# Batched x·yᵀ on one core: PSUM copies of 4 banks and a last load in one piece

## The chip, the core and the metric

The kernel runs on one core of a Trainium2 chip. The metric is the device time of one execution in microseconds (us). The kernel before took 305.55 us, the median of three runs (304.52 to 305.66). The execution that the profiler recorded has a span of 303.9 us from its first to its last event.

## The reference

```python
def setup_inputs():
    batch, n_heads, seq_t, seq_s, channels = 8, 12, 512, 512, 64
    # x: [8, 12, 512, 64] fp32, y: [8, 12, 512, 64] fp32

def reference(x, y):
    return np.einsum('bhtc,bhsc->bhts', x, y).astype(np.float32)
```

For each of the 96 heads the product of a 512x64 matrix with the transpose of another is formed. The inputs are 25 MB, the output is 101 MB.

## The kernel before

The heads are taken in 12 load groups of 8. In a group x and y are each a block of 128 rows of 8 KB. A loaded group is turned into bf16 (`compress`), x is spread into buffers that are zero elsewhere (`mix`), both are transposed on VectorE (`transposes`), and `result` multiplies, copies the product out of PSUM and returns its store. There are 48 output tiles of 2 MB (128 partitions x 4096 fp32).

All large buffers, the loaded groups and the output tiles alike, come from one pool of five slots, taken in turn: whoever takes a slot waits until the one that had it five turns earlier is done with it.

```python
    slots = ctx.enter_context(tc.tile_pool(name="slots", bufs=SLOTS))          # SLOTS = 5
    pm3pool = ctx.enter_context(tc.tile_pool(name="pm3psum", bufs=2, space=bass.MemoryType.PSUM))
    pm2pool = ctx.enter_context(tc.tile_pool(name="pm2psum", bufs=1, space=bass.MemoryType.PSUM))

    def load(g):
        both = slot()
        for src, dst in ((xv[g], both[:, :R * C]), (yv[g], both[:, R * C:])):
            cuts = (0, P) if g < NG - 1 else (0, P - 16, P - 12, P - 8, P - 4, P)
            for lo, hi in zip(cuts[:-1], cuts[1:]):
                nc.sync.dma_start(dst[lo:hi], src[lo:hi])
        loaded[g] = both
```

Eleven groups are loaded with one DMA for x and one for y. The last is loaded with five DMAs each: rows 0 to 111, and four times 4 rows.

```python
    def result(o):
        i, h = divmod(o, 2)
        xT, yT = made[i]
        otf = slot()
        ot = otf.rearrange("p (r s) -> p r s", s=S)
        for k, n in ((0, 3), (3, 3), (6, 2)):
            pm = (pm3pool if n == 3 else pm2pool).tile([P, n, S], fp32, name=f"pm{n}")
            for j in range(n):
                nc.tensor.matmul(
                    pm[:, j, :], xT[:, k + j, h, :], yT[:, h * S:(h + 1) * S], start=True, stop=True
                )
            copy(nc.vector if o % 4 == 3 else nc.scalar, ot[:, k:k + n, :], pm)
        # ... transposes or mix for a later tile
        return lambda: nc.sync.dma_start(ov[i, h], otf)
```

[...] a tile fills eight banks[...]. Of four tiles ScalarE copies three and VectorE one.

```python
        for g in range(SLOTS):
            load(g)
        for k in range(0, K * E * D, 64):                       # K * E * D = 1024
            nc.vector.memset(zeroed[0][:, k:k + 64], 0.0)
            nc.gpsimd.memset(zeroed[1][:, k:k + 64], 0.0)
        stores = []
        for g in range(NG):                                     # NG = 12
            compress(g)
            mix(g // 2, [nc.gpsimd] * 4, (g % 2,))
            if g in (2, 4):
                transposes(g // 2 - 1)
            if g < 5:
                load(g + SLOTS)
            elif g in (5, 7, 9):
                stores.append(result(len(stores)))
            elif g in (6, 8):
                load(g // 2 + 7)
        for store in stores:
            store()
        for o in range(len(stores), 4 * NG):
            result(o)()
```

Three output tiles are thus made while the loads still run. Their stores are issued after the last load, all from SyncE's queue, and from then on each tile is stored when it is made.

Of the kernel before, what the change touches and what calls it, by code (L numbers as in the profile page):

```python
# [1 line left out]

# [4 lines left out]


@with_exitstack
def kernel(  # L10
    ctx: ExitStack,
    tc: tile.TileContext,
    x: bass.AP,
    y: bass.AP,
    out: bass.AP,
):

    nc = tc.nc
    B, H, T, C = x.shape  # L30
    _, _, S, _ = y.shape
    P = 128
    G = 8
    Q = P // G
    R = T // Q
    NG = B * H // G
    K = 8
    E = R // K
    D = 32
    SLOTS = 5  # L40
    fp32 = mybir.dt.float32
    bf16 = mybir.dt.bfloat16
    u32 = mybir.dt.uint32
    COPY = mybir.ActivationFunctionType.Copy
    assert C == 2 * D and S == T and R == D and Q * 2 == D

    xv = x.rearrange("b h t c -> (b h t c)").rearrange("(g p n) -> g p n", p=P, n=R * C)
    yv = y.rearrange("b h t c -> (b h t c)").rearrange("(g p n) -> g p n", p=P, n=R * C)
    ov = out.rearrange("b h t s -> (b h t s)").rearrange(
        "(o u h q n) -> o h q u n", u=2, h=2, q=Q * E, n=K * S  # L50
    )

    const = ctx.enter_context(tc.tile_pool(name="const", bufs=1))
    kept = ctx.enter_context(tc.tile_pool(name="kept", bufs=NG))
    slots = ctx.enter_context(tc.tile_pool(name="slots", bufs=SLOTS))
    tpool = ctx.enter_context(tc.tile_pool(name="tpool", bufs=3))
    pm3pool = ctx.enter_context(tc.tile_pool(name="pm3psum", bufs=2, space=bass.MemoryType.PSUM))
    pm2pool = ctx.enter_context(tc.tile_pool(name="pm2psum", bufs=1, space=bass.MemoryType.PSUM))

    loaded, inputs, mixed, made = {}, {}, {}, {}  # L60
    zeroed = [const.tile([P, K * E * D], u32, name=f"xb{half}") for half in range(2)]
    in_front = [nc.vector, nc.gpsimd, nc.vector, nc.scalar]
    FIRST = NG // 2

    def copy(engine, dst, src):
        if engine is nc.scalar:
            nc.scalar.activation(dst, src, COPY)  # L67
        else:
            engine.tensor_copy(dst, src)  # L69

    def slot():
        return slots.tile([P, K * S], fp32, name="slot")

    def load(g):
        both = slot()
        for src, dst in ((xv[g], both[:, :R * C]), (yv[g], both[:, R * C:])):
            cuts = (0, P) if g < NG - 1 else (0, P - 16, P - 12, P - 8, P - 4, P)
            for lo, hi in zip(cuts[:-1], cuts[1:]):
                nc.sync.dma_start(dst[lo:hi], src[lo:hi])  # L79
        loaded[g] = both  # L80

    def compress(g):

        both = loaded.pop(g)
        xk = kept.tile([P, R, C], bf16)
        nc.scalar.activation(xk.rearrange("p r c -> p (r c)"), both[:, :R * C], COPY)  # L86
        inputs[g] = xk
        ys = both[:, R * C:].rearrange("p (r c) -> p r c", c=C)
        for half in range(2):
            yb = kept.tile([P, R // 2 * D], u32, name=f"yb{half}")  # L90
            yv2 = yb.bitcast(bf16).rearrange("p (j c w) -> p j w c", j=R // 2, w=2)
            for ch in range(2):
                copy(
                    in_front[2 * half + ch],
                    yv2[ch * 64:(ch + 1) * 64],
                    ys[half * 64:(half + 1) * 64, :, ch * D:(ch + 1) * D].rearrange(
                        "p (j w) c -> p j w c", w=2
                    ),
                )
            mixed[2 * g + half] = yb  # L100

    def mix(i, engines, halves=(0, 1)):

        g, half = divmod(i, 2)
        xk = inputs[g]
        xv2 = zeroed[half].bitcast(bf16).rearrange("p (k e c u) -> p k e c u", k=K, e=E, u=2)
        for ch in halves:
            for u in range(2):
                lo = half * 64 + u * D
                copy(  # L110
                    engines[2 * ch + u],
                    xv2[(2 * ch + u) * D:(2 * ch + u + 1) * D, :, :, :, u],
                    xk[lo:lo + D, :, ch * D:(ch + 1) * D].rearrange("p (e k) c -> p k e c", k=K),
                )

    def transposes(i):
        xb, yb = zeroed[i % 2], mixed.pop(i)
        xT = tpool.tile([P, K * D * E], u32)
        nc.vector.transpose(  # L119
            xT.rearrange("p (k r e) -> p k e r", k=K, e=E),  # L120
            xb.rearrange("p (k e c) -> p k e c", k=K, e=E),
        )
        yT = tpool.tile([P, D * R // 2], u32)
        nc.vector.transpose(  # L124
            yT.rearrange("p (r j) -> p j r", r=D), yb.rearrange("p (j c) -> p j c", c=D)
        )
        made[i] = (xT.bitcast(bf16).rearrange("p (k h m) -> p k h m", k=K, h=2), yT.bitcast(bf16))

    def result(o):

        i, h = divmod(o, 2)
        xT, yT = made[i]
        otf = slot()
        ot = otf.rearrange("p (r s) -> p r s", s=S)
        for k, n in ((0, 3), (3, 3), (6, 2)):
            pm = (pm3pool if n == 3 else pm2pool).tile([P, n, S], fp32, name=f"pm{n}")
            for j in range(n):
                nc.tensor.matmul(  # L138
                    pm[:, j, :], xT[:, k + j, h, :], yT[:, h * S:(h + 1) * S], start=True, stop=True
                )  # L140
            copy(nc.vector if o % 4 == 3 else nc.scalar, ot[:, k:k + n, :], pm)
        if h == 0 and i + 2 < 2 * NG:
            transposes(i + 2)
        elif h == 1 and FIRST <= i + 4 < 2 * NG:
            mix(i + 4, [nc.scalar if o % 4 == 3 else nc.vector] * 4)
        return lambda: nc.sync.dma_start(ov[i, h], otf)

    with tc.manual_schedule():
        for g in range(SLOTS):
            load(g)  # L150
        for k in range(0, K * E * D, 64):
            nc.vector.memset(zeroed[0][:, k:k + 64], 0.0)  # L152
            nc.gpsimd.memset(zeroed[1][:, k:k + 64], 0.0)  # L153
        stores = []
        for g in range(NG):
            compress(g)
# [15 lines that stand above are left out]
# [1 line left out]
_INS = ['x', 'y']  # L173
_OUTS = [((8, 12, 512, 512), 'float32')]


# [23 lines left out]
```

## Time and profile before

| what | value |
|---|---|
| time, median of 3 | 305.55 us |
| span of the profiled execution | 303.9 us |
| granted TensorE clock, mean | 0.71 |
| ScalarE busy | 221.5 us |
| VectorE busy | 181.3 us |
| TensorE busy | 146.2 us |
| GpSimd busy | 59.1 us |
| moved by DMA | 125.93 MB, 414 GB/s over the span |
| time from issue to landing, stores (median) | 19.6 us |

In the profile a group of instructions is named by its line, engine and operation, then output<-input with shapes, the count, the busy time and the mean of one, and after the second bar the idle time of that engine just before these instructions with what ended it. The helper `copy` is one line for several uses (L67 on ScalarE, L69 on the other engines), so its groups are told apart by tile names and shapes: `slot<-pm` is a copy out of PSUM, `yb<-slot` and `xb<-xk` belong to the preparation. SPq is SyncE's queue of DMA issues: L79 issues loads and L146 stores. In rows by stage the columns are the stretch, its length, the busy time of PE, PEld, DVE, ACT and POOL with the number of instructions, then the granted clock, the mean busy share of the 16 DMA engines and the GB/s that they moved. A DMA engine counts as busy as long as it has a packet under way, however long that takes.

### The profile page before, as it was taken

To read this page: it belongs to the slowest core of one execution; us is meant where nothing else is said; L and a number is where in the kernel's file an instruction comes from. 1 tells how busy PE (TensorE), PEld (TensorE's weight loads), DVE (VectorE), ACT (ScalarE), POOL (GpSimd) and SP (SyncE) were. 2 spreads that over 40 slices of the span, in tenths; PEclk is the share of its full clock that TensorE was granted. 3 is DMA by queue.
4 is the path that set the end of the run, shared out by engine and by line. 5 is a ranking of instruction groups with operands and counts; after the bars stand their busy time and mean duration, and the time that the engine had idled before them with its cause. 6 is when DMAs were issued, how large, how long until landed. Compare 5 with 4: busy or idle time off the path is not lost.

```text
span 303.9 us, 1432 instructions
## 1 busy us (share of the span) xinstructions
PE 146.2 (48%) x384; PEld 46.5 (15%) x384; DVE 181.3 (60%) x160; ACT 221.5 (73%) x169; POOL 59.1 (19%) x56
## 2 busy tenths in 40 slices
PE   0004044225648457574757467565575477475000
PEld 0001011001212112121212112121121122121000
DVE  1568895909997493883947919569196461502300
ACT  4566599975998978979789888798896977184000
POOL 2899999945000000000000000000000000000000
PEclk9999555555995985776675965778857965776655
DMA  7999999999999999999999999999999999999995
GB/s 289 426 424 422 424 421 423 360 294 437 426 427 429 418 436 423 429 430 425 434 427 421 438 418 427 434 423 434 429 423 434 426 425 429 424 429 431 421 440 250
DMA packets 10409, 125.93 MB, mean 414 GB/s; under 512 B 1184, under 2 KB 1184, under 8 KB 1184
## 3 DMA queue, kind: packets, MB, share of 16 engines
q1 hardware_dynamic: 10400, 125.83, 99.0%
q8 instruction: 3, 0.05, 0.1%
q14 instruction: 6, 0.05, 0.0%
HBM read 25.17 MB, written 100.66 MB: 414 GB/s over the span
## 4 chain that ended last, share of the span: by engine, by line
DMA 62%; ACT 17%; DVE 8%; issue 4%; PE 1%; DVEq 1%; SPq 0%; ACTq 0%
DMA out_dram<-slot 49%; ACT slot L67 12%; DMA slot<-in_y_dram 11%; DVE slot L69 5%; DMA slot<-in_x_dram 3%; ACT xk L86 2%; ACT xb L67 2%; DVE yb L69 2%; ACT yb L67 1%; PE pm L138 1%; DVE xT L119 1%; DVE yT L124 1%; DVEq L195 1%; SPq L79 0%; DVEq L69 0%
## 5 line engine op out<-in xcount | busy, mean ns | idle before, releaser
L138 PE MATMUL pm<-yT,xT 128*128 128x512 bf16 x384 | 146.2, 521 | 133.0 <-ACT slot L67 74.5
L67 ACT ACTIVATE slot<-pm 128x1536 f32<-128x1536 f32 (+1 forms) x108 | 133.4, 1311 | 39.3 <-DMA out_dram<-slot 27.9
L69 DVE COPY slot<-pm 128x1536 f32<-128x1536 f32 (+1 forms) x36 | 54.6, 1572 | 73.0 <-DMA out_dram<-slot 40.6
L138 PEld LDWEIGHTS <-xT 128*128 128x128 bf16 x384 | 46.5, 121 | 231.8 <-issue 197.5
L119 DVE STREAM_TRANSPOSE xT<-xb 128x1024 uint32<-128x1024 uint32 x24 | 49.4, 2056 | 4.7 <-PE pm L138 3.1
L67 ACT ACTIVATE xb<-xk 32x1024 bf16<-32x1024 bf16 x36 | 48.1, 1337 | 0.8
L69 DVE CAST yb<-slot 64x1024 bf16<-64x1024 f32 x24 | 31.9, 1328 | 23.5 <-DMA slot<-in_y_dram 23.3
L69 POOL COPY xb<-xk 32x1024 bf16<-32x1024 bf16 x24 | 38.1, 1586 | 1.2
L86 ACT ACTIVATE xk<-slot 128x2048 bf16<-128x2048 f32 x12 | 22.9, 1910 | 9.9 <-DMA slot<-in_x_dram 9.4
L69 DVE COPY xb<-xk 32x1024 bf16<-32x1024 bf16 x36 | 26.1, 725 | 0.4
L124 DVE STREAM_TRANSPOSE yT<-yb 128x512 uint32<-128x512 uint32 x24 | 25.5, 1062 | 0.0
L69 POOL CAST yb<-slot 64x1024 bf16<-64x1024 f32 x12 | 19.7, 1643 | 11.5 <-DMA slot<-in_y_dram 10.9
L67 ACT ACTIVATE yb<-slot 64x1024 bf16<-64x1024 f32 x12 | 16.0, 1329 | 5.6 <-DMA slot<-in_y_dram 5.4
L86 ACT ACT_TABLE_LOAD x1 | 1.3, 1283 | 0.7 <-PEq L184 0.7
L152 DVE MEMSET xb<- 128x64 uint32 x16 | 1.2, 112 | 0.8 <-PEq L184 0.8
L153 POOL MEMSET xb<- 128x64 uint32 x16 | 1.4, 151 | 0.3 <-POOLq L184 0.3
L184 POOL MEMSET const-float32-0.0<- 128x1 f32 x1 | 0.1, 98 | 0.2 <-issue 0.2
L184 POOL MEMSET const-float32-1.0<- 128x1 f32 x1 | 0.1, 98 | 0.0
L184 POOL MEMSET const-bfloat16-1.0<- 128x1 bf16 x1 | 0.1, 98 | 0.0
L184 POOL MEMSET const-uint8-127<- 128x1 uint8 x1 | 0.1, 98 | 0.0
## 6 DMA issues: line engine op xcount, KB each, us to landing
out_dram<-slot SPq DMA_DIRECT2D x48, 2048.0 KB, 19.6
slot<-in_x_dram SPq DMA_DIRECT2D x11, 1024.0 KB
slot<-in_y_dram SPq DMA_DIRECT2D x11, 1024.0 KB, 19.9
slot<-in_x_dram SPq DMA_DIRECT2D x1, 896.0 KB
slot<-in_y_dram SPq DMA_DIRECT2D x1, 896.0 KB, 11.2
slot<-in_x_dram SPq DMA_DIRECT2D x4, 32.0 KB
slot<-in_y_dram SPq DMA_DIRECT2D x4, 32.0 KB
```

The source lines that it names most:

```text
L67: nc.scalar.activation(dst, src, COPY)
L69: engine.tensor_copy(dst, src)
L86: nc.scalar.activation(xk.rearrange("p r c -> p (r c)"), both[:, :R * C], COPY)
L119: nc.vector.transpose(xT.rearrange("p (k r e) -> p k e r", k=K, e=E), xb.rearrange("p (k e c) -> p k e c", k=K, e=E),)
L124: nc.vector.transpose(yT.rearrange("p (r j) -> p j r", r=D), yb.rearrange("p (j c) -> p j c", c=D))
L138: nc.tensor.matmul(pm[:, j, :], xT[:, k + j, h, :], yT[:, h * S:(h + 1) * S], start=True, stop=True)
L152: nc.vector.memset(zeroed[0][:, k:k + 64], 0.0)
L153: nc.gpsimd.memset(zeroed[1][:, k:k + 64], 0.0)
L184: nc = _bacc.Bacc("TRN2", target_bir_lowering=False, num_devices=1)
L195: with _tile.TileContext(nc) as tc:
```

## The change

It has three parts. The output tile leaves PSUM in two copies of four banks instead of three copies of 3, 3 and 2 banks, with one PSUM pool of two buffers in place of two pools with three buffers, so that there are fewer and larger copies. VectorE sets its buffer to zero in 4 fills of 256 columns instead of 16 of 64 (GpSimd keeps its 16), which makes 20 in all. And the last load group is loaded like the others, with one DMA of 128 rows for x and one for y, in place of the ten pieces.

```diff
-    pm3pool = ctx.enter_context(tc.tile_pool(name="pm3psum", bufs=2, space=bass.MemoryType.PSUM))
-    pm2pool = ctx.enter_context(tc.tile_pool(name="pm2psum", bufs=1, space=bass.MemoryType.PSUM))
+    pmpool = ctx.enter_context(tc.tile_pool(name="pmpsum", bufs=2, space=bass.MemoryType.PSUM))
 ...
     def load(g):
         both = slot()
-        for src, dst in ((xv[g], both[:, :R * C]), (yv[g], both[:, R * C:])):
-            cuts = (0, P) if g < NG - 1 else (0, P - 16, P - 12, P - 8, P - 4, P)
-            for lo, hi in zip(cuts[:-1], cuts[1:]):
-                nc.sync.dma_start(dst[lo:hi], src[lo:hi])
+        nc.sync.dma_start(both[:, :R * C], xv[g])
+        nc.sync.dma_start(both[:, R * C:], yv[g])
         loaded[g] = both
 ...
-        for k, n in ((0, 3), (3, 3), (6, 2)):
-            pm = (pm3pool if n == 3 else pm2pool).tile([P, n, S], fp32, name=f"pm{n}")
-            for j in range(n):
+        for k in range(0, K, 4):
+            pm = pmpool.tile([P, 4, S], fp32)
+            for j in range(4):
                 nc.tensor.matmul(
                     pm[:, j, :], xT[:, k + j, h, :], yT[:, h * S:(h + 1) * S], start=True, stop=True
                 )
-            copy(nc.vector if o % 4 == 3 else nc.scalar, ot[:, k:k + n, :], pm)
+            copy(nc.vector if o % 4 == 3 else nc.scalar, ot[:, k:k + 4, :], pm)
 ...
-        for k in range(0, K * E * D, 64):
-            nc.vector.memset(zeroed[0][:, k:k + 64], 0.0)
-            nc.gpsimd.memset(zeroed[1][:, k:k + 64], 0.0)
+        for half, engine, part in ((0, nc.vector, 256), (1, nc.gpsimd, 64)):
+            for k in range(0, K * E * D, part):
+                engine.memset(zeroed[half][:, k:k + part], 0.0)
```

## The prediction

> **What bounds the kernel now.** I first read the busy shares on the page, then the 40 slices with the DMA and GB/s rows.
>
> ```profile
> PE 146.2 (48%) x384; PEld 46.5 (15%) x384; DVE 181.3 (60%) x160; ACT 221.5 (73%) x169; POOL 59.1 (19%) x56
> ...
> DMA  7999999999999999999999999999999999999995
> GB/s 289 426 424 422 424 421 423 360 294 437 426 427 429 418 436 423 429 430 425 434 427 421 438 418 427 434 423 434 429 423 434 426 425 429 424 429 431 421 440 250
> DMA packets 10409, 125.93 MB, mean 414 GB/s; under 512 B 1184, under 2 KB 1184, under 8 KB 1184
> ...
> HBM read 25.17 MB, written 100.66 MB: 414 GB/s over the span
> ```
>
> No compute engine is above 73%, while the DMA row is 9 in 38 of 40 slices. The span is set by moving 125.83 MB at some 425 GB/s: 125.83 MB / 0.425 = 296 us of the 303.9. What can be won at all lies in the four slices that fall short: the first and the last, and the two in the middle with 360 and 294 GB/s. In those two the DMA row still says 9: the DMA engines are occupied but move less. That is the line that decides this case.
>
> Next, the table by stage around that dip (columns: busy time of PE, PEld, DVE, ACT, POOL, then granted clock, DMA share, GB/s):
>
> ```profile
> 54.00:58.00 4.00, 0.00 (x0) 0.00 (x0) 3.97 (x3) 3.87 (x4) 3.84 (x3) 0.50 1.02 393
> 58.00:60.00 2.00, 0.90 (x3) 0.34 (x3) 1.99 (x3) 2.00 (x2) 1.73 (x1) 0.50 1.04 299
> 60.00:62.00 2.00, 2.00 (x6) 0.61 (x5) 0.68 (x1) 1.98 (x3) 1.90 (x3) 0.50 1.15 229
> 62.00:64.00 2.00, 0.74 (x2) 0.15 (x1) 0.00 (x0) 1.98 (x2) 1.22 (x1) 0.50 0.92 184
> 64.00:66.00 2.00, 0.00 (x0) 0.00 (x0) 0.00 (x0) 1.69 (x2) 0.00 (x0) 0.50 0.99 365
> 66.00:68.00 2.00, 0.00 (x0) 0.00 (x0) 0.68 (x1) 0.81 (x1) 0.65 (x1) 0.50 0.99 406
> ...
> 76.00:300.00 224.00, 127.90 (x341) 40.63 (x340) 130.96 (x109) 167.40 (x134) 0.00 (x0) 0.72 1.01 428
> 300.00:303.90 3.90, 0.00 (x0) 0.00 (x0) 0.00 (x0) 0.00 (x0) 0.00 (x0) 0.50 0.19 80
> ```
>
> From 54 to 68 us the rate falls to 184 GB/s and comes back. Against 425 GB/s each row loses (1 - rate/425) x its length: 0.30 + 0.59 + 0.92 + 1.13 + 0.28 + 0.09 = 3.3 us of full transfer. What runs then is shown by SyncE's own timeline, which issues every transfer:
>
> ```profile
> 54.27 1.74 SPq L79 DMA_DIRECT2D slot<-in_x_dram  x5
> 56.06 6.65 SPq L79 DMA_DIRECT2D slot<-in_y_dram  x5
> 63.31 2.64 SPq L146 DMA_DIRECT2D out_dram<-slot  x3
> ```
>
> This is the last load group, the one in ten pieces. SyncE needs until 62.7 us to issue the pieces, and the first store, whose data has been in SBUF since 40.6 us, is only issued at 63.31. The trace's DMA packet records add the cause of the low rate. A row of 8 KB takes 0.31 us (median) in all loads before; of the 224 packets of the two 112-row transfers, nearly all take 0.42 to 1.03 us, mean 0.55, from 57.4 until 65 us. Then four engines still have 8 KB rows of the small pieces until 68.4 us, while the other twelve start the first store at 64.9.
>
> [...] 72 transfers x 16 + 8 pieces x 4 = 1184, which is the count of packets under 512 B above. [...]
>
> **The change part by part.** *1. The copies out of PSUM.* From the groups with shapes kept apart (the number after "busy us" is the mean ns of one):
>
> ```profile
> L67 ACT ACTIVATE slot<-pm 128x1536 f32<-128x1536 f32 x72 | 100.7, 1450 | 39.3 <-DMA out_dram<-slot 27.9 <-PE pm L138 4.0 <-DVE slot L69 2.9
> L67 ACT ACTIVATE slot<-pm 128x1024 f32<-128x1024 f32 x36 | 37.2, 1034 | 0.0
> L69 DVE COPY slot<-pm 128x1536 f32<-128x1536 f32 x24 | 41.0, 1751 | 73.0 <-DMA out_dram<-slot 40.6 <-PE pm L138 32.4
> L69 DVE COPY slot<-pm 128x1024 f32<-128x1024 f32 x12 | 14.6, 1214 | 0.0
> ...
> L152 DVE MEMSET xb<- 128x64 uint32 x16 | 1.2, 112 | 0.8 <-PEq L184 0.8
> ```
>
> A bank costs 1450 - 1034 = 416 ns on ScalarE and 537 ns on VectorE. A copy of 4 banks should take 1450 + 416 = 1.87 us on ScalarE and 2.29 us on VectorE. A tile goes from 3.93 to 3.73 us on ScalarE (36 tiles: 7 us less busy) and from 4.72 to 4.58 us on VectorE (12 tiles: 1.7 us less). Against it, there are two PSUM buffers instead of three, so TensorE fills 4 banks while the other 4 are emptied: 4 matmuls at the slower spacing seen, 0.43 us, are 1.7 us, still under the copy's 1.87. A store lasts 100.66 MB / 48 / 0.428 = 4.9 us per tile, longer than any copy of a tile. The waits above show that the copies already wait for stores (40.6 us on VectorE, 27.9 on ScalarE). All of part 1 therefore lies beside the transfers: 0 us.
>
> *2. The zeros.* VectorE's 16 small fills (1.2 us) become 4, and GpSimd keeps 16. VectorE then waits for the first y until 8.1 us. 0 us.
>
> *3. The last load group whole.* It removes eight transfers and puts 128 rows on 16 engines again. At 0.31 us a row, 8 rows of x and 8 of y take 4.95 us per engine: from 57.4 to 62.4 us instead of 64.9 on twelve engines and 68.2 on four. SyncE issues x and y by 55 us and can issue two stores right after, so each engine goes from the last load row to the first store row without a gap. Twelve engines gain 2.5 us, four gain 5.8 us; weighted, (12 x 2.5 + 4 x 5.8) / 16 = 3.3 us, the same as the table's loss.
>
> Does it stay won? The third store's tile leaves ScalarE at about 61.3 us, the fourth can be copied when the first store has landed (62.4 + 4.9 + 1, about 68.3) and takes 4.6 us: ready at 73 us. The three stores before it keep the engines busy until 62.4 + 3 x 4.9 = 77 us. The margin is 4 us, then it grows. At the end the last store is issued at 283.7 us, long before its turn, so the tail is a pure drain, and the gain comes out there. What the whole program gains depends on which engines end last: the twelve give 2.5, the four up to 5.8. The packet records show the engines' last completions between 300.6 and 302.95 us, and my attempt to follow engines through the records suggests that the four late ones are among the last. I take 3.5 us, a little above the mean.
>
> Sum: 0 + 0 + 3.5. 305.55 - 3.5 = 302.0 us.
>
> **The rivals.** *A: the dip is only shifted.* If the first stores after the load find no finished tile, the engines run dry at 73 us instead. For it: only three tiles are made ahead, and the fourth has 4 us of margin. Against it: slots and copies have that margin and VectorE, which copies it, idles before. If true, 0 to 2 us gain, 304 us. *B: two PSUM buffers of 4 banks make compute the bound.* For it: TensorE waits for PSUM already (74.5 us on ScalarE's copies). Against it: 4.2 us per tile even with a handoff of 0.2 per copy is below 4.9, and the order of ScalarE's work in four tiles (3 x 3.73 + 4 x 1.34 = 16.5 us) is below 4 x 4.9. If true, the DMA row would fall below 9 in the middle: 306 to 312 us. *C: the pieces were good for the tail.* They give twelve engines 14 rows instead of 16, 0.62 us less each; if those are the slow engines, the whole load gives that back. This is inside my sum for the twelve already and leaves at least 2.5 us.
>
> **Range and chances.** The low end takes 5 us of gain (four late engines set the end): 300.6. The high end takes 1.7 (some of A, plus the spread of the runs before, 304.52 to 305.66): 303.8. Faster by 2% needs under 299.4, a gain of 6.1 us, more than the whole dip; chance 0.05. Slower by 2% needs B; 0.01. Within 2%: 0.94.
>
> **What would show it.** Right: slices 8 and 9 of the GB/s row at about 425 and no ten-piece load; stores issued from 55 us; 72 transfers x 16 = 1152 packets under 512 B; ScalarE copies of 2048 elements near 1.87 us; a first store landing near 68 us. Wrong: a low GB/s slice somewhere between 73 and 90 us (A), DMA digits of 8 or less in the middle (B), or a last slice much emptier than 250 GB/s (C).

## The result, and the profile after

The changed kernel takes 302.0 us (median of 6 runs, 301.59 to 302.08) against 305.32 us; the ratio is 0.9893, with a 95% interval of 0.9879 to 0.9906. By the 2% mark that is the same time, and yet a clear gain of 3.3 us. The span of the profiled execution went from 303.9 to 300.3 us.

The same rows of the page, after (DMA busy tenths, GB/s in 40 slices, packets, totals):

```profile
DMA  7999999999999999999999999999999999999994
GB/s 282 430 422 421 420 423 422 421 432 443 420 432 438 417 434 437 421 437 434 420 437 434 423 432 432 423 443 426 421 450 419 426 439 423 419 437 428 426 434 194
DMA packets 10375, 125.92 MB, mean 419 GB/s; under 512 B 1152, under 2 KB 1152, under 8 KB 1152
...
HBM read 25.17 MB, written 100.66 MB: 419 GB/s over the span
```

The two slices of 360 and 294 GB/s are now 421 and 432, and nothing has dipped in their place. The DMA digits have hardly changed: they were 9 in the dip and are 9 now. Only the GB/s row shows the difference. The small packets are 32 fewer, four for each of the eight pieces.

By stage, over the same stretches (columns as before: PE, PEld, DVE, ACT, POOL, clock, DMA share, GB/s):

```profile
54.00:58.00 4.00, 0.00 (x0) 0.00 (x0) 3.97 (x3) 3.87 (x4) 3.88 (x3) 0.68 1.02 426
58.00:60.00 2.00, 0.56 (x2) 0.25 (x2) 1.99 (x3) 2.00 (x2) 1.96 (x1) 0.50 1.01 418
60.00:62.00 2.00, 2.00 (x6) 0.55 (x4) 0.56 (x1) 1.98 (x2) 1.93 (x2) 0.50 1.05 434
62.00:64.00 2.00, 0.76 (x3) 0.24 (x2) 0.63 (x1) 1.98 (x2) 1.70 (x2) 0.92 1.05 446
...
76.00:296.00 220.00, 123.70 (x336) 39.92 (x334) 126.09 (x92) 162.39 (x99) 0.00 (x0) 0.71 1.01 430
```

And SyncE's timeline around the last load, then the groups of the copies and of VectorE's zeros:

```profile
54.19 0.33 SPq L74 DMA_DIRECT2D slot<-in_x_dram  x1
54.57 0.42 SPq L75 DMA_DIRECT2D slot<-in_y_dram  x1
55.04 23.12 SPq L142 DMA_DIRECT2D out_dram<-slot  x6
```

```profile
L65 ACT ACTIVATE slot<-pm 128x2048 f32<-128x2048 f32 x72 | 131.1, 1876 | 40.0 <-DMA out_dram<-slot 31.6 <-PE pm L134 3.5 <-DVE yb L67 2.6
L67 DVE COPY slot<-pm 128x2048 f32<-128x2048 f32 x24 | 53.8, 2285 | 70.3 <-DMA out_dram<-slot 49.0 <-issue 19.8 <-PE pm L134 1.5
...
L149 DVE MEMSET xb<- 128x256 uint32 x4 | 1.1, 272 | 0.9 <-PEq L180 0.9
```

The last load is issued at the same time as before, 54.2 us, but it takes 0.8 us to issue instead of 8.4, and the first store follows at 55.04 instead of 63.31. In the DMA packet records the first rows of the first store start between 62.0 and 62.9 us on all 16 engines; before it was 64.6 to 65.0 us on twelve and 67.4 to 68.2 us on four. (These times are in the clock of the lines above; the packet times in the prediction lie about 0.24 us higher, which cancels in its differences.)

### The profile page after: what moved, and what is told of

It reads as the page before. It is cut to its first block, busy times and chain, and to the rows that moved or that the text cites. A ratio compares the mean times of both kernels' runs of the same rounds, so it can differ in the third digit from the quotient of the medians.

```text
span 300.3 us, 1359 instructions
## 1 busy us (share of the span) xinstructions
PE 143.4 (48%) x384; PEld 46.3 (15%) x384; DVE 180.8 (60%) x136; ACT 219.2 (73%) x133; POOL 59.3 (20%) x56
## 4 chain that ended last, share of the span: by engine, by line
DMA 49%; ACT 13%; DVE 5%; issue 4%; PE 1%; DVEq 1%; ACTq 0%
DMA out_dram<-slot 49%; ACT slot L65 10%; DVE slot L67 4%; ACT xb L65 2%; PE pm L134 1%; DVEq L191 1%; ACT xk L82 1%; DVE yb L67 0%; ACT yb L65 0%; DVE yT L120 0%; DVEq L67 0%; ACTq L65 0%
## 5 line engine op out<-in xcount | busy, mean ns | idle before, releaser
L134 PE MATMUL pm<-yT,xT 128*128 128x512 bf16 x384 | 143.4, 519 | 132.5 <-ACT slot L65 78.1
L65 ACT ACTIVATE slot<-pm 128x2048 f32<-128x2048 f32 x72 | 131.1, 1876 | 40.0 <-DMA out_dram<-slot 31.6
L67 DVE COPY slot<-pm 128x2048 f32<-128x2048 f32 x24 | 53.8, 2285 | 70.3 <-DMA out_dram<-slot 49.0
L67 DVE CAST yb<-slot 64x1024 bf16<-64x1024 f32 x24 | 32.7, 1362 | 19.0 <-DMA slot<-in_y_dram 18.7
L149 DVE MEMSET xb<- 128x256 uint32 x4 | 1.1, 272 | 0.9 <-PEq L180 0.9
## 6 DMA issues: line engine op xcount, KB each, us to landing
slot<-in_x_dram SPq DMA_DIRECT2D x12, 1024.0 KB, 17.6
```

Of the source, the lines that this page charges most:

```text
L134: nc.tensor.matmul(pm[:, j, :], xT[:, k + j, h, :], yT[:, h * S:(h + 1) * S], start=True, stop=True)
L149: engine.memset(zeroed[half][:, k:k + part], 0.0)
```

## The experiments

My theory: the last load is the whole difference, and it was slow because a row of it takes longer (0.55 us in the mean for the 112-row DMAs, against 0.31 in the whole groups), by where the rows of such a DMA lie in SBUF. Rivals: the copies carry a part of it; the ten small DMAs and their late issue are the cause, not the rows; or what counts is where the rows lie in HBM and not in SBUF. Each run below is one edit of one of the two kernels.

**1. The last load alone.** The kernel before, with

```diff
-            cuts = (0, P) if g < NG - 1 else (0, P - 16, P - 12, P - 8, P - 4, P)
+            cuts = (0, P)
```

> The kernel before with one edit: the last load group whole. If the last load is the whole change (my theory): 302.0 us, the dip of the GB/s row gone, the copies still 3, 3 and 2 banks. If the copies out of PSUM or the zeros carry part of it (rival; 16 KB store packets took 615.5 ns on average before and 612.8 after, which over 384 packets per engine is 1 us): about 303 us.

Measured: 302.08 us, ratio 0.9887 (0.9869 to 0.9904) to the kernel before.

**2. The other two parts alone.** The changed kernel with the ten pieces put back:

> The changed kernel with the ten pieces of the last load put back, so the copies of 4 banks and the 20 zero fills alone. My theory: 305.3 us like before, with the dip between 57 and 68 us. Rival (copies carry part): about 304.3 us. The two runs together must add up to the whole difference of 3.3 us.

Measured: 305.19 us, ratio 0.9991 (0.9981 to 1.0000). The GB/s rows of the two runs, experiment 1 first; the dip of slices 8 and 9 goes with the load in one piece and comes back with the ten pieces:

```profile
GB/s 289 427 419 426 421 428 419 419 442 429 419 448 421 419 450 421 421 450 419 427 445 419 430 439 419 432 441 419 441 428 421 439 431 419 422 426 441 423 423 203
GB/s 290 425 425 419 425 420 423 367 292 428 434 420 436 419 430 430 426 431 428 421 437 424 428 426 430 421 437 426 424 434 426 426 432 426 424 434 421 434 426 285
```

The two add up within the noise, and the division is clean: the load is the whole gain, copies and zeros together are at most 0.2%. In the first run the copies are still the old ones and cost what they cost before:

```profile
L67 ACT ACTIVATE slot<-pm 128x1536 f32<-128x1536 f32 x72 | 100.8, 1453 | 38.2 <-DMA out_dram<-slot 31.6 <-DVE yb L69 2.6 <-issue 1.9
```

They wait 31.6 us for stores, as the new ones do (31.6 in the group above). The 7 us of busy time that the larger copies save on ScalarE (137.9 us before, 131.1 after) do not reach the end.

**3. Four DMAs instead of ten, but 112 rows.** The changed kernel, last load in two DMAs each for x and y (only the line with the cuts is shown):

```diff
+            cuts = (0, P) if g < NG - 1 else (0, P - 16, P)
```

> The changed kernel with the last load of 112 rows and one DMA of 16 rows, for x and y, so four DMAs instead of ten[...]. If the loss of before came from the small pieces (four engines with most of the rows, and the issue of ten DMAs which delays the stores to 63.3 us): stores issued by 56 us, 8 KB packets at 0.31 us, 302.2 us. If it came from 112 rows [...]: packets of 0.4 to 0.6 us again from 57.4 us, the last load takes 7 to 8.5 us instead of 4.95, 304 to 305.5 us although the stores are issued early.

Measured: 305.37 us, ratio 0.9995 (0.9984 to 1.0006). SyncE's timeline and the stages:

```profile
55.94 21.25 SPq L144 DMA_DIRECT2D out_dram<-slot  x5
```

```profile
58.00:60.00 2.00, 0.62 (x2) 0.25 (x2) 1.87 (x3) 2.00 (x2) 1.50 (x1) 0.50 1.05 291
60.00:62.00 2.00, 2.00 (x6) 0.59 (x5) 0.90 (x1) 1.98 (x2) 1.94 (x2) 0.50 1.03 197
62.00:64.00 2.00, 1.02 (x3) 0.26 (x2) 0.00 (x0) 1.98 (x2) 1.41 (x2) 0.50 0.99 279
64.00:66.00 2.00, 0.00 (x0) 0.00 (x0) 0.00 (x0) 1.98 (x2) 0.00 (x0) 0.50 1.09 299
```

The stores are issued early, at 55.94 us, no four engines are late any more (the first rows of the first store start at 64.9 to 66.0 us; with the pieces at 64.6 to 65.0 on twelve engines and 67.4 to 68.2 on four), and the whole loss is still there. The engines are busy (shares near 1) at 197 to 299 GB/s, half to two thirds of the rate: slow packets (0.49 us in the middle, against 0.31), not missing ones. Those first rows start some 3 us later than in the changed kernel. So the slow rows alone are enough for the loss.

**4. Other cuts, in earlier groups.** The changed kernel with four groups cut differently (again only the line with the cuts):

```diff
+            cuts = {3: (0, 64, P), 5: (0, 96, P), 7: (0, 32, 64, 96, P), 9: (0, 112, P)}.get(g, (0, P))
```

> The changed kernel with four earlier load groups cut in other ways: group 3 in 64 + 64 rows, group 5 in 96 + 32, group 7 in four times 32, group 9 in 112 + 16. Read from the 8 KB packets and the GB/s by stage. [...] packets of 0.62 us and some 215 GB/s in groups 3 and 7 (9.9 us per group), 96 + 32 about 8 us, 112 + 16 about 8.3 us; together some 17 us more than the changed kernel, about 318 us. If only the row count 112 or small pieces matter: groups 3, 5 and 7 at 0.31 us and 425 GB/s, about 303 us.

Measured: 319.62 us (one run). The stages of groups 3, 5, 7 and 9 and, last, of two whole groups:

```profile
18.00:27.00 9.00, 3.25 (x8) 1.24 (x9) 6.04 (x5) 3.24 (x2) 6.27 (x5) 1.00 1.01 218
33.00:41.00 8.00, 0.00 (x0) 0.00 (x0) 5.68 (x5) 3.24 (x2) 5.09 (x4) 0.50 1.01 240
47.00:56.00 9.00, 1.78 (x5) 0.48 (x4) 5.64 (x5) 5.04 (x3) 6.10 (x4) 0.50 1.00 219
61.00:69.50 8.50, 2.77 (x7) 0.79 (x6) 2.59 (x3) 5.99 (x4) 4.84 (x3) 0.70 1.01 244
70.00:78.00 8.00, 3.63 (x8) 1.09 (x8) 7.27 (x6) 7.27 (x5) 7.41 (x5) 0.50 1.01 421
```

In groups 3 and 7 an 8 KB packet takes about 0.61 us, twice 0.31, and the rate is half, 218 and 219 GB/s against 421 in the two whole groups. The extra 17.6 us over the changed kernel are close to my estimate (17); why a row of these cuts takes twice as long, the run does not show. Nothing is special about 112 (244 GB/s with 16 more rows) or about small pieces: 64 + 64 rows are slower.

**5. SBUF or HBM.** Is it where the rows lie in SBUF, or where they come from? Group 3 now has 64 rows from 32 to 95 in one DMA, where experiment 4 had rows 0 to 63. One run, three groups (cut to the table of rows):

```diff
+        rows = {
+            3: ((32, 96), (0, 32), (96, P)),
+            5: ((0, 112), (112, P)),         # source: every second row of groups 6 and 7
+            8: ((16, P), (0, 16)),
+        }.get(g, ((0, P),))
```

> The changed kernel with three load groups cut in other ways. Group 3: rows 32 to 95 first, then 0 to 31, then 96 to 127. Group 5: 112 + 16 rows, the source being every second row of groups 6 and 7, so the partitions are those of the runs before and the HBM addresses are others (the products of group 5 are then of other rows). Group 8: rows 16 to 127, then 0 to 15. [...] 0.31 us per packet although it is a DMA of 64 rows, which took 0.62 us for rows 0 to 63; the two DMAs of 32 rows stay at 0.62; group 3 takes 7.4 us. Group 5 stays slow at 0.45 to 0.95 us per packet, 8 to 9 us, whatever the source. Group 8 is slow too, about 8 us. Theory of the source [...]: rows 32 to 95 at 0.62 us as well, and group 5 fast or of another speed.

Measured: 313.25 us (one run; the output of group 5 is that of other rows). The stages: rows 32 to 95 of x; the two DMAs of 32 rows of x; rows 32 to 95 of y; its DMAs of 32 rows; group 5; group 8.

```profile
17.80:18.60 0.80, 0.00 (x0) 0.00 (x0) 0.49 (x1) 0.49 (x1) 0.73 (x2) 1.00 1.03 430
19.00:22.00 3.00, 0.00 (x0) 0.00 (x0) 2.97 (x2) 0.43 (x1) 2.90 (x3) 1.00 0.97 216
22.00:23.00 1.00, 0.00 (x0) 0.10 (x1) 1.00 (x2) 0.66 (x1) 1.00 (x1) 1.00 1.23 393
23.00:26.00 3.00, 2.48 (x6) 0.86 (x6) 1.10 (x2) 1.25 (x1) 0.73 (x2) 1.00 0.97 218
31.00:39.50 8.50, 0.00 (x0) 0.00 (x0) 5.32 (x4) 3.24 (x2) 4.82 (x3) 1.00 1.03 241
...
50.00:58.50 8.50, 2.99 (x7) 0.95 (x7) 3.04 (x3) 7.39 (x5) 4.89 (x3) 1.00 1.02 248
```

The same number of rows, 64, runs at 393 to 430 GB/s from row 32 (an 8 KB packet takes 0.31 to 0.32 us there in the middle) and at 218 from row 0. And with the HBM addresses changed, 112 + 16 rows are as slow (241) as in experiment 4 (244). By these two the cause is where the rows lie in SBUF. What it is about their place that slows them was not shown: the packet records do not name engines, and which rows an engine gets is not seen. One miss of size: 112 + 16 rows take 8.7 us in experiment 4 and 9.0 us here, where I had estimated 8.3, and group 3 takes 8.2 us instead of 7.4 (from the group's first row to the first row of the second group after it, less the 4.97 us of the whole group between). Where the rest comes from stays open.

**6. Ten DMAs, but of 128 rows.** The last load cut by columns:

```diff
+        cuts = (0, R * C) if g < NG - 1 else (0, 1024, 1280, 1536, 1792, 2048)
+        for src, at in ((xv[g], 0), (yv[g], R * C)):
+            for lo, hi in zip(cuts[:-1], cuts[1:]):
+                nc.sync.dma_start(both[:, at + lo:at + hi], src[:, lo:hi])
```

> The changed kernel with the last load again in ten DMAs, but cut by columns: x and y each 128 rows by 1024 columns and four times 128 rows by 256 columns. [...] If the ten DMAs themselves (their issue, their completions) cost time: 303 to 305 us. If only the rows per DMA matter: 302.0 to 302.5 us, the small rest for packets of 1 KB.

Measured: 302.71 us, ratio 0.9909 (0.9889 to 0.9929) to the kernel before, so 0.7 us above the changed kernel's 302.0, a little more than the 0.5 that I had expected at most; measured against the kernel before, which ran beside it at 305.62 us, the gain is 2.9 us instead of 3.3. SyncE's timeline:

```profile
59.92 2.69 SPq L144 DMA_DIRECT2D out_dram<-slot  x3
```

The ten DMAs hold the first store back until 59.92 us, but the load's packets last until 62.4 us on the first engine and 63.4 us on the last, so no engine runs dry. What is lost lies in the smaller packets: 4 KB takes 0.163 us and 1 KB 0.046, so a row in five packets takes 0.35 us instead of 0.31, about 0.5 us over 16 rows. Ten DMAs by rows lose 3.3 us, ten by columns 0.4 to 0.7.

**7. Late stores alone.** The changed kernel with eight tiny loads between the last load and the first store:

```diff
+        if g == NG - 1:
+            for n in range(8):
+                nc.sync.dma_start(tiny[n], xv[0][:16, :32])
```

> The changed kernel with eight tiny loads (16 rows of 128 B, to buffers that nobody reads) issued between the last load and the first store. At most eight DMAs are under way at once in the traces, so the first store is issued only when the tiny loads begin to land, at about 63.3 us as in the kernel before, while the last load runs at full rate. If the late issue of the stores costs by itself: the engines run dry from 62.4 us to 64.8 us, 302 + 2.4 + 0.3 for the tiny loads, about 304.7 us. If the issue has no weight of its own: 302.3 us.

Measured: 305.25 us, ratio 0.9993 (0.9982 to 1.0004). SyncE's timeline and the stages:

```profile
55.01 8.63 SPq L79 DMA_DIRECT2D tiny<-in_x_dram  x8
63.69 2.64 SPq L146 DMA_DIRECT2D out_dram<-slot  x3
```

```profile
60.00:62.00 2.00, 2.00 (x6) 0.57 (x5) 1.66 (x1) 1.98 (x2) 1.96 (x2) 0.50 0.97 398
62.00:64.00 2.00, 1.04 (x3) 0.27 (x2) 0.66 (x1) 1.98 (x2) 1.47 (x2) 0.50 0.08 11
64.00:66.00 2.00, 0.00 (x0) 0.00 (x0) 1.99 (x3) 1.98 (x2) 1.94 (x2) 0.50 0.63 263
```

Here the load is as fast as in the changed kernel, and the engines then stand still: a share of 0.08 at 11 GB/s. By the packet records the standstill is 2.9 us per engine, where I had worked out 2.4; that is the miss of 0.5 us. Compare the dip of the kernel before, 0.92 to 1.15 at 184 to 229 GB/s. Two quite different states of the DMA engines cost the same 3 us.

In the kernel before it is the slow rows alone that cost the time. Its stores too are issued late, at 63.31 us, but the slow rows keep the engines occupied: between 54 and 76 us they stand idle for 0.15 us per engine, by the packet records (0.02 in experiment 2, which has the same pieces). The late issue lies in the shadow of the slow rows, and comes to light once the rows are fast, as here. So mending only one of the two gains nothing (experiment 3 mends the issue, and this run has fast rows with a late issue); the whole load mends both.

## Why the prediction was right

The time was foreseen as 302.0 us and is 302.0. The mechanism is the one foreseen; that the number is met to the tenth is in part luck, as the last step shows. By its steps:

- **The dip as the place of the gain**: right. The dip of 3.3 us is gone, and experiment 1 shows that the load alone brings the whole gain.
- **The copies**: 1.87 and 2.29 us foreseen, 1.876 and 2.285 measured; off the path as foreseen (experiment 2). Two PSUM buffers of four banks (a bank is here the 512 fp32 per partition that one matmul writes) did not become the bound: the stage from 76 us moves 430 GB/s.
- **The zeros**: 4 fills take 1.1 us where 16 took 1.2, and nothing waits for them.
- **The last load**: end at 62.4 us and stores by 55 us foreseen; 62.0 to 62.9 and 55.04 measured. What makes its rows slow the prediction did not show; by experiments 4 and 5 it is where they lie in SBUF (218 GB/s for rows 0 to 63, 393 to 430 for rows 32 to 95). What the prediction did not see is that the slow rows and the late issue each suffice. Its sum started from where the rows were seen to end, so it held, but "take away either" would have been a wrong forecast.
- **The margin of the fourth store**: wrong in path and size, on the safe side. The prediction let its copy wait for the first store to land, about 68.3 us. VectorE's timeline (start, length, what) shows it right after the casts of the last load:

```profile
63.37 2.49 DVE L67 CAST yb<-slot 64x1024 bf16<-64x1024 f32 x2 [2.82 <-DMA slot<-in_y_dram]
65.76 4.46 DVE L67 COPY slot<-pm 128x2048 f32<-128x2048 f32 x2
```

  The first store lands at 67.8 us, two microseconds after this copy began, so the tile does not have the first store's slot, as taking five slots in turn would give it. The wait ahead of the copy in VectorE's queue ends at 64.48 us, when ScalarE has turned the last part of load group 10 into bf16 (63.12 to 64.44 us): the tile has that group's slot. A wait for the first store's semaphore stands ahead of the sixth tile only (72.19 us). This fits a pool that hands slots on in the order in which the program is done with them, and the program stores its three early tiles only after load groups 10 and 11. Ready at 70.2 us, the tile has a margin of 6.4 us before its store's first row at 76.6, not 4; rival A had even less room than I gave it.
- **The tail**: half right. The packet records give each engine's last completion. Their mean went from 301.1 to 296.5 us, 4.6 us; the last one went from 302.71 to 298.95, only 3.8. Two things are in this that the sum did not have. The 16 KB rows of the stores became faster, 612.8 ns against 615.5, which is 1.0 us over the 384 rows of an engine. And the end became less even: one engine now ends 2.7 us after the middle of the sixteen; before it was 1.8. The last slice is emptier (194 against 250 GB/s), which was the sign named for rival C. The two nearly cancel, which is the luck in the number; besides, the kernel before came out at 305.32 us over six runs, not 305.55, so that the gain is 3.3 us and not 3.5. Whether the pieces had helped the tail is not shown: experiment 3, with equal rows on all engines, ends its last engine 3.2 us after the middle, and experiment 7 1.5.

## What to carry to other kernels

Read the GB/s row beside the DMA busy row: a busy DMA engine at half the rate (a share of 0.92 to 1.15 at 184 to 229 GB/s in the kernel before) is a different fault from an idle one (0.08 at 11 GB/s in experiment 7), and the first can hide the second. Here a 128-row transfer cut by columns (302.71 us) cost less than one cut by rows (305.19 us); rows 32 to 95 alone kept the rate (393 to 430 GB/s), rows 0 to 63 did not (218), so measure a cut by rows before keeping it. Put nothing small ahead of the stores where the program limits the DMAs under way: in the trace of the changed kernel never more than eight are under way (the ninth is issued at 5.67 us, when the first has landed at 5.65), and in experiment 7 eight tiny loads hold SyncE from 55.01 to 63.64 us. A fault can lie in the shadow of another one at the same time; then mending one of them shows nothing, so test each alone on the good kernel, not only on the bad one.

## What the runs showed of the hardware that I had not expected

The 16 KB rows of the stores do not go at one pace. Their mean from 76 us on is 612.8 ns in the changed kernel and 613.0 in experiment 1, but 615.5 in the kernel before and 615.3 in experiment 2, so the pace goes with the last load and not with the copies. It is 611.8 in experiment 3 and 616.7 in experiment 7, where all engines start the first store within 0.15 us of each other (0.9 us in the changed kernel). Over 384 rows 4 ns are 1.5 us. No run was made for that alone, and the cause stays open.

In the changed kernel, in experiment 1 and in experiment 3 the last engine of a store falls behind the middle of the sixteen by degrees, from 0.5 to 0.7 us at the first stores to 2.7 to 3.2 us at the last, with the same rows as the rest. With the ten pieces it is the other way round: 3.3 us at the first store and 1.8 at the last in the kernel before, 3.5 and 1.2 in experiment 2. Which engine it is, and why, the records don't tell.
